# Reversed SSM tables by eight whole copies, and a step of the table batches every 5.5 ticks in a macaron decoder layer

## The chip, the cores and the metric

The kernel runs on one core of one Trainium2 chip. The metric is the device time of one execution in microseconds (us). The engines are PE (TensorE, matmuls), DVE (VectorE), ACT (ScalarE), POOL (GpSimd) and SP (SyncE, which here only issues DMAs). Each engine works through its own instructions in order and waits on semaphores for the others.

## The reference, cut to what matters

One decoder layer on 1024 tokens of width 1024, all in f32:

```
x = x + 0.5 * g1 * swiglu(modulate(rms_norm(x), sh1, sc1), W_gate, W_up, W_down)      # FFN1, width 2816
b, c, v, u = split(modulate(rms_norm(x), sh2, sc2) @ w_in)
yA = b * conv3_causal(c * v)
yB = GLU(Re(C . state) + D * u)      # state_t = Abar * state_{t-1} + Bbar * u_t, 32 groups of 16 channels, 64 states
x = x + g2 * ([rms_norm(yA) | rms_norm(yB)] @ w_out)
x = x + 0.5 * g3 * swiglu(modulate(rms_norm(x), sh3, sc3), ...)                       # FFN2
y = rms_norm_final(x)
```

`Abar = exp(lambda * dt)` and `Bbar = (Abar - 1) / lambda * B` come from the inputs, so the tables that the SSM (state space) stage needs can be made long before that stage. The state recursion is done in blocks of 8 time steps, and needs the powers 0 to 8 of `Abar`, once in rising and once in falling order.

## The kernel before, in words

Every product in f32 is made of three matmuls on fp32r operands split in a high and a low part (`mm3`, one *tick*). ACT casts a weight tile to its high part, DVE subtracts to get the low part (`w<-raw,w`). FFN1 and FFN2 use a seven-product scheme for blocks of two by two: the eleven groups of FFN1 are named fa0 to fa10, and groups fa2 to fa10 run through `seven`, first its side g (gate), then its side u (up). A side is seven steps of twelve matmuls (four ticks) into PSUM banks in the order A, C, B, D, A, E, C. In the trace they are `fa8gA`, `fa8gC` and so on. DVE adds the banks up (`fa8gu`, `fa8gt`, `fa8ut`); the second C accumulates onto the first one's bank, so PE may begin it only when DVE has added the first C in (`fa3gt<-fa3gu,fa3gC`). At the end of side u some ten more additions make the group's products and their sums (X, Y, Z, W).

Work that isn't part of FFN1 itself lies in a generator, `side1`, which `clock.tick` moves on by one `yield` after every `clock.period` ticks. It makes, in this order, the seven-product operands, the bases of the SSM tables (`ssm_base`) and the tables in eight batches of four groups (`ssm_batch`):

- `ssm_base` has the powers of `Abar` in `pw` (128 partitions, 2 parts, 9 powers, 32 groups) and makes four tables from it, `tab0` to `tab3`. The lower and upper 64 partitions take different parts and signs. `tab0` and `tab1` are whole copies (64x288); `tab2` and `tab3` have the powers 7 to 0 in reverse, copied one power at a time (64x32). After each of the eight table halves stands a `yield`.
- `ssm_batch(b)` makes, on DVE, `bb`, `cl`, `bl` and the rotors `rot`/`rott`. `bl` is a product with `tab2`, to which `blt`, a product with `tab3`, is added. Later steps put two small groups of work on PE, `kp` (reads `bl` and `cl`) and `tp` (transposes `bl`), and evacuate them (`kc`, `mi`). Each batch has 15 DMAs on SP: its parameters `prm`, and stores to `mo_d`, `co_d`, `si_d`, `mk_d` (eight) and `mi_d`. The batches also take eight `wm` tiles of the modulation along, all of them near the first one.

The period is 4.5 ticks from group fa2 on (`clock.period = 4.5`). When group fa10 begins, what is left of `side1` is run off, its buffers are closed, and the x tiles for the residual take their place (`load_x`); so the x loads wait for the last batch's stores. After FFN1's first half of the down projection the period is set to 8.

The rows of most instructions carry line L108, that of a recording wrapper; they are told apart by their tile names. The order of instructions on each engine is set by a scheduler from data dependences and its own estimates, in the neighbourhood of where they were written.

Of the kernel before, what the change touches and what calls it, by code (L numbers as in the profile page):

```python
# [13 lines left out]
F32 = mybir.dt.float32  # L14
F32R = mybir.dt.float32r
I32 = mybir.dt.int32
AF = mybir.ActivationFunctionType
# [4 lines left out]
P = 128  # L22
# [8 lines left out]
G = 32  # L31
# [201 lines left out]
def hymba_layer(ctx: ExitStack, tc, x_d, wm1_d, wmod_d, gu1_d, gs1_d, ds1_d, wl1_d, win_d, wout_d, glu_d, gu2_d, gs2_d, wd2_d, ds2_d, wl2_d, cols_d, cond_d, lam_d, bc_d, out_d):  # L233
    nc = tc.nc
    V, A, T, SP = (InOrder(tc, e) for e in (nc.vector, nc.scalar, nc.tensor, nc.sync))
# [82 lines left out]
    clock = Clock(4)  # L318
# [143 lines left out]
    def mod_fetch(home):  # L462
        if home is not None:
            n, b, i = later.pop(0)
            r = home(f"wm{n}_{b}_{i}")
            SP.dma_start(r, wmod_d[n - 2, b, :, i, :])
            fetched.append((n, 2 * b + i, r))
# [350 lines left out]
    for h in range(2):  # L818
# [7 lines left out]
        q = sqs[0]  # L826
# [94 lines left out]
    def ssm_base(sb, sb1):  # L921
# [102 lines left out]
        pw = sb1.tile([P, 2, 9, G], F32, tag="pw", name="pw")  # L1024
# [10 lines left out]
        yield  # L1035

        tabs = [sb.tile([P, 9, G], F32, tag=f"tab{i}", name=f"tab{i}") for i in range(4)]
        for n, (t, (top, ts_, bot, bs_)) in enumerate(zip(tabs, ((0, 1, 1, -1), (1, -1, 0, -1), (0, 1, 1, 1), (1, -1, 0, 1)))):
            for part, i, sg in ((lo, top, ts_), (hi, bot, bs_)):
                if n < 2:  # L1040
                    A.activation(t[part], pw[part, i], AF.Copy, scale=float(sg))
                else:

                    for q in range(8):
                        A.activation(t[part, q, :], pw[part, i, 7 - q, :], AF.Copy, scale=float(sg))
                yield
        zero = sb1.tile([CH, 112], F32, name="zero")
        V.memset(zero[:], 0.0)
        mk4 = mk_d[:].rearrange("b p (g c) -> p b g c", g=GB)
# [105 lines left out]
    def combos1():  # L1155

        sh = mods[:, 0, :]
        both = const.tile([P, 4], F32, name="both")
        V.tensor_tensor(out=both[:], in0=sh[:, :4], in1=sh[:, 4:], op=ALU.add)
        blocks.clear()  # L1160
        blocks.update(A11=act1[0][:4], A12=act1[0][4:], A22=act1[1][4:], S1=[], S2=[], S3=[], S4=[])
        for k in range(4):
            (t11, t21), (t12, t22) = x[k], x[4 + k]
            V.scalar_tensor_tensor(out=t22, in0=t22, scalar=both[:, k : k + 1], in1=t21, op0=ALU.add, op1=ALU.add)
            blocks["S1"].append(split_act(t22, f"h1S1_{k}", "B"))
            yield
            V.tensor_tensor(out=t21, in0=t11, in1=t21, op=ALU.subtract)
            blocks["S3"].append(split_act(t21, f"h1S3_{k}", "B"))
            yield
            V.scalar_tensor_tensor(out=t11, in0=t22, scalar=sh[:, k : k + 1], in1=t11, op0=ALU.subtract, op1=ALU.subtract)  # L1170
            blocks["S2"].append(split_act(t11, f"h1S2_{k}", "B"))
            yield
            V.scalar_tensor_tensor(out=t12, in0=t12, scalar=sh[:, 4 + k : 5 + k], in1=t11, op0=ALU.add, op1=ALU.subtract)
            yield
        while not left_free:
            yield
        for k in range(4):
            blocks["S4"].append(split_act(x[4 + k][0], f"h1S4_{k}", "A"))
            yield
        xp_open.close()  # L1180
        first_opened()

    def side1():
        yield from combos1()
        sb = side_open.enter_context(tc.tile_pool(name="sb", bufs=1, side="right"))
        with tc.tile_pool(name="sb1", bufs=1, side="right") as sb1:
            yield from ssm_base(sb, sb1)
        bps.append(side_open.enter_context(tc.tile_pool(name="bp", bufs=1, side="right")))
        mod_home.pool = side_open.enter_context(tc.tile_pool(name="wmp", bufs=1, side="right"))
        for _ in range(2):  # L1190
            mod_fetch(mod_home)
        for b in range(NB):
            yield from ssm_batch(b)
# [20 lines left out]
    def gate_up(act, name, kept, last):  # L1214

        afs = {}
        for fi in range(2):
            if last and fi:
                wg, wu = ws.take(2)
                for h in (1, 0):  # L1220
                    pg, pu = proj(wg, act[h], f"{name}g{fi}_{h}"), proj(wu, act[h], f"{name}u{fi}_{h}")
                    gu_keep(fi, h, pg, pu, afs, kept, name)
                    if h:
                        left_free.append(True)
                        clock.period = LAST_PERIOD
                ws.free(2)
# [7 lines left out]
            ws.free()  # L1234

    movs["B"] = es1.enter_context(tc.tile_pool(name="movB1", bufs=12))
    LAST_PERIOD = 2
    sums_open, first_open = ExitStack(), ExitStack()

    def first_opened():  # L1240
# [2 lines left out]
    ws.sums_pool = sums_open.enter_context(tc.tile_pool(name="sums", bufs=2))  # L1243
    ws.pump()
    clock.side.append(side1())
    clock.period = 3.5
    for g in range(1, SEVEN_FROM[0]):
# [483 lines left out]
```

## Time and profile before

| | |
|---|---|
| median of 3 runs | 1735.42 us (1735.38 to 1735.46) |
| the profiled execution, its own time | 1740.78 us |
| its span in the trace | 1739.0 us |
| mean granted TensorE clock | 0.987 |
| PE busy | 1665.4 us, 96% of the span |
| DVE busy | 1273.6 us, 73% |
| ACT busy | 596.7 us, 34% |
| POOL busy | 375.9 us, 22% |

A row of the timeline has the start in us from the span's begin, the length in us, the engine, the line, the operation, outputs and inputs by the program's names, the shape, and how many instructions are merged in the row; in square brackets, where the engine stood idle ahead of it, for how long and what ended that. Lengths of neighbouring rows overlap by about 0.1 us, so paces are taken from start to start. Busy shares are means over stages with different limits; FFN1, where the change lies, fills the trace from about 50 to 725 us.

### The profile page before, as it was taken

Reading aid. Unit: us, or ns where it says so; the run is one execution under the profiler, and the core shown is the slowest. Engines: PE = TensorE matmul, PEld = TensorE weight load, DVE = VectorE, ACT = ScalarE, POOL = GpSimd, SP = SyncE. Lnnn points to the kernel's source line nnn. Section 1 sums busy time; section 2 is a strip of 40 time slices with the busy share of each in tenths; the row PEclk is TensorE's granted clock in tenths of the full one; section 3 lists DMA queues with packets and bytes.
Section 4 is the critical chain, followed back from the end, with each engine's and each line's share of the span. In section 5 each row is a group of like instructions: output and inputs, shape, how many; then the busy total and the mean of one; then the engine's idle time right before and its main releaser. Section 6 shows DMA issues by size and latency. Waiting matters only on the chain.

```text
span 1739.0 us, 20621 instructions
## 1 busy us (share of the span) xinstructions
PE 1665.4 (96%) x7484; PEld 1368.4 (79%) x7484; DVE 1273.6 (73%) x2014; ACT 596.7 (34%) x1016; POOL 375.9 (22%) x290
## 2 busy tenths in 40 slices
PE   4999999999999999999999999999999999999997
PEld 3787788878878878787777778778888888888886
DVE  7939699997589997634556977967777766676656
ACT  4225433333364332331113414424444443322221
POOL 0012233322322222100000022123223322333211
PEclk9999999999999999999999999999999999999998
DMA  8222464554464656134655450114445334659312
GB/s 326 78 99 91 146 217 150 158 183 150 182 224 147 230 198 238 53 98 142 198 152 155 134 182 25 49 49 157 167 187 186 152 145 170 248 236 365 119 49 97
DMA packets 98167, 275.17 MB, mean 158 GB/s; under 512 B 18961, under 2 KB 34577, under 8 KB 86930
## 3 DMA queue, kind: packets, MB, share of 16 engines
q1 hardware_dynamic: 98066, 273.86, 44.8%
q8 instruction: 59, 0.97, 0.2%
q14 instruction: 42, 0.34, 0.1%
HBM read 194.65 MB, written 74.97 MB: 155 GB/s over the span
## 4 chain that ended last, share of the span: by engine, by line
PE 46%; DVE 7%; DMA 3%; issue 1%; ACT 0%; SPq 0%; POOL 0%; DVEq 0%; ACTq 0%
PE wo L108 2%; PE fb10d L108 2%; PE u L108 2%; PE fbd_1B L108 2%; PE fbd_0B L108 2%; PE b L108 2%; DMA swz<-si 1%; PE v L108 1%; PE fb0g L108 1%; PE fbd_1C L108 1%; PE fbd_0C L108 1%; PE fbd_1A L108 1%; PE fbd_0A L108 1%; DVE x L108 1%; DMA wm<-in_wmod 1%; PE gl L108 1%
## 5 line engine op out<-in xcount | busy, mean ns | idle before, releaser
L108 ACT CAST w<-raw 128x512 fp32r<-128x512 f32 (+1 forms) x374 | 240.4, 677 | 475.8 <-issue 79.4
L108 DVE TENSOR_TENSOR w<-raw,w 128x512 fp32r<-128x512 f32 (+1 forms) x374 | 306.6, 839 | 122.3 <-ACT w L108 121.7
L174 POOL TENSOR_TENSOR raw<-sums,raw 128x512 f32<-128x512 f32 x54 | 80.4, 1490 | 416.4 <-DVE w L108 404.0
L165 POOL TENSOR_TENSOR sums<-raw 128x512 f32<-128x512 f32 x54 | 77.4, 1434 | 335.5 <-DMA raw<-in_gs 140.8
L176 POOL TENSOR_TENSOR raw<-raw 128x512 f32<-128x512 f32 x54 | 84.7, 1571 | 96.5 <-DVE w L108 96.5
L166 POOL TENSOR_TENSOR raw<-raw 128x512 f32<-128x512 f32 x54 | 85.3, 1579 | 4.2
L108 DVE CUSTOM_DVE_ANT_0 wm<-wm,cact 128x1024 f32<-128x1024 f32 x56 | 77.6, 1398 | 10.6 <-DMA wm<-in_wmod 10.5
L367 POOL TENSOR_TENSOR n3aq<-n3aq,n3aq 128x512 f32<-128x512 f32 x5 | 7.7, 1530 | 281.3 <-ACT n3aq L108 281.1
L108 PE MATMUL p<-h,w 128*128 128x512 f32 x192 | 48.5, 415 | 8.2 <-DVE h L108 5.4
L108 DVE TENSOR_TENSOR w<-sums,w 128x512 fp32r<-128x512 f32 x54 | 52.7, 988 | 3.0 <-ACT w L108 2.4
L108 PEld LDWEIGHTS p<-h,w 128*128 128x128 f32 x192 | 38.4, 202 | 18.0 <-DVE h L108 6.4
L108 PE MATMUL wo<-oa,w 128*128 128x512 f32 x192 | 46.0, 392 | 1.2 <-DVE w L108 0.7
L108 PE MATMUL v<-h,w 128*128 128x512 f32 x192 | 46.8, 395 | 0.0
L108 PE MATMUL c<-h,w 128*128 128x512 f32 x192 | 46.6, 394 | 0.0
L108 PE MATMUL u<-h,w 128*128 128x512 f32 x192 | 46.3, 401 | 0.2 <-DVE h L108 0.2
L108 PE MATMUL b<-h,w 128*128 128x512 f32 x192 | 45.6, 393 | 0.0
L108 PE MATMUL wo<-ob,w 128*128 128x512 f32 x192 | 45.3, 391 | 0.0
L108 ACT CAST w<-sums 128x512 fp32r<-128x512 f32 x54 | 32.8, 620 | 35.2 <-PE fa9gE L108 2.2
L108 PEld LDWEIGHTS u<-h,w 128*128 128x128 f32 x192 | 36.7, 193 | 8.6 <-DVE h L108 0.6
L108 PEld LDWEIGHTS wo<-oa,w 128*128 128x128 f32 x192 | 35.7, 188 | 9.6 <-DVE w L108 1.1
L108 PEld LDWEIGHTS wo<-ob,w 128*128 128x128 f32 x192 | 35.8, 188 | 7.3
L108 PEld LDWEIGHTS b<-h,w 128*128 128x128 f32 x192 | 35.5, 188 | 7.2
(1576 smaller groups left out, 4013.1 us busy)
## 6 DMA issues: line engine op xcount, KB each, us to landing
raw<-in_gs SPq DMA_DIRECT2D x38, 1024.0 KB, 5.2
wm<-in_wmod SPq DMA_DIRECT2D x56, 512.0 KB, 4.8
raw<-in_ds SPq DMA_DIRECT2D x16, 1024.0 KB, 6.0
mw<-in_wm SPq DMA_DIRECT2D x8, 1024.0 KB, 12.8
x<-in_x SPq DMA_DIRECT2D x16, 512.0 KB, 8.5
raw<-in_win SPq DMA_DIRECT2D x8, 1024.0 KB, 5.1
raw<-in_gu SPq DMA_DIRECT2D x6, 1024.0 KB, 10.0
raw<-in_wl SPq DMA_DIRECT2D x5, 1024.0 KB, 6.5
```

The source lines that it names most:

```text
L108: r = getattr(self.engine, name)(*args, **kw)
L165: self.G.tensor_tensor(out=f, in0=r[2], in1=r[1], op=ALU.subtract)
L166: self.G.tensor_tensor(out=r[1], in0=r[1], in1=r[0], op=ALU.subtract)
L174: self.G.tensor_tensor(out=r, in0=s["t3"], in1=r, op=ALU.add)
L176: self.G.tensor_tensor(out=r, in0=self.chunk(j, 3), in1=r, op=ALU.subtract)
L367: nc.gpsimd.tensor_tensor(out=a, in0=a, in1=sq[:, :n], op=ALU.add)
```

## The change

In `ssm_base` the falling powers are first copied whole, both parts and all partitions at once, into a new tile `pd` (eight copies of 128x2x32, a `yield` after the fourth and the eighth). Then `tab2` and `tab3` take their halves from it in one instruction each (64x256, four in all). A `yield` stands behind each table, no longer behind each half, so the tables have six of them (two of the copies) in place of eight. When `ssm_base` is through, `side1` sets the period to 5.5 ticks for the batches.

```diff
         tabs = [sb.tile([P, 9, G], F32, tag=f"tab{i}", name=f"tab{i}") for i in range(4)]
+        down_ = sb1.tile([P, 2, 8, G], F32, tag="pd", name="pd")
+        for q in range(8):
+            A.copy(down_[:, :, q, :], pw[:, :, 7 - q, :])
+            if q % 4 == 3:
+                yield
         for n, (t, (top, ts_, bot, bs_)) in enumerate(...):
             for part, i, sg in ((lo, top, ts_), (hi, bot, bs_)):
                 if n < 2:
                     A.activation(t[part], pw[part, i], AF.Copy, scale=float(sg))
                 else:
-                    for q in range(8):
-                        A.activation(t[part, q, :], pw[part, i, 7 - q, :], AF.Copy, scale=float(sg))
-                yield
+                    A.activation(t[part, 0:8, :], down_[part, i], AF.Copy, scale=float(sg))
+            yield
...
             yield from ssm_base(sb, sb1)
+        clock.period = BATCH_PERIOD
...
-    LAST_PERIOD = 2
+    LAST_PERIOD, BATCH_PERIOD = 2, 5.5
```

How that changes the order of the built program, at three places. First ACT in side g of group fa3, where the tables are made. `w_1344` and `w_1400` are weight tiles that are cast, `fa3gt` is the side's activation. Before:

```order
L108 ACTIVATE tab_1523<-pw 64x288
L108 ACTIVATE tab_1524<-pw 64x288
L108 ACTIVATE tab_1523<-pw 64x288
L108 CAST w_1344<-raw_1039 128x512
L108 CAST w_1344<-raw_1165 128x512
L108 ACTIVATE tab_1524<-pw 64x288
L108 ACTIVATE tab_1525<-pw 64x32 x16
L108 ACTIVATE tab_1526<-pw 64x32 x16
L108 CAST w_1400<-raw_1165 128x512 x2
L108 ACTIVATE fa3gt_1321<-fa3gt_1321 128x512
```

and after:

```order
L108 ACTIVATE tab_1523<-pw 64x288
L108 ACTIVATE tab_1524<-pw 64x288
L108 COPY pd<-pw 128x2x32 x2
L108 CAST w_1344<-raw_1039 128x512
L108 CAST w_1344<-raw_1165 128x512
L108 COPY pd<-pw 128x2x32 x6
L108 ACTIVATE tab_1523<-pw 64x288
L108 ACTIVATE tab_1524<-pw 64x288
L108 ACTIVATE tab_1525<-pd 64x256 x2
L108 ACTIVATE tab_1526<-pd 64x256 x2
L108 CAST w_1400<-raw_1165 128x512 x2
L108 ACTIVATE fa3gt_1321<-fa3gt_1321 128x512
```

The casts keep their places; between `w_1344` and `w_1400` stand 12 instructions where there were 33.

Second, DVE around the seventh batch's `bl`. The rows from the end of group fa7 (`fa7Y`) to the last addition into `bl_3172`, before:

```order
L108 TENSOR_TENSOR fa7Y<-fa7uu_3025,fa7gu_2837 128x512
L108 TENSOR_TENSOR cl_3140<-tab_1523,prm_3131 128x576
L108 TENSOR_TENSOR clt_3141<-tab_1524,prm_3131 128x576
L108 TENSOR_TENSOR fa7W<-fa7Y,fa7W 128x512
L108 TENSOR_TENSOR w_3158<-raw_2822,w_3158 128x512 x2
L108 TENSOR_TENSOR cl_3140<-cl_3140,clt_3141 128x576
L108 TENSOR_TENSOR w_3205<-raw_2822,w_3205 128x512
L108 TENSOR_TENSOR bl_3172<-tab_1525,bb_3133 128x512
L108 TENSOR_TENSOR w_3205<-raw_2986,w_3205 128x512
L108 TENSOR_TENSOR blt_3173<-tab_1526,bb_3133 128x512
L108 TENSOR_TENSOR fa8gu_3232<-fa8gt_3182,fa8gB 128x512
L108 TENSOR_TENSOR bl_3172<-bl_3172,blt_3173 128x512
```

The seventh batch's `bl_3284` after, half a group on, behind the last addition of side g of fa8:

```order
L108 TENSOR_TENSOR fa8gu_3151<-fa8gu_3151,fa8gC 128x512
L108 TENSOR_TENSOR cl_3257<-cl_3257,clt_3258 128x576
L108 TENSOR_TENSOR bl_3284<-tab_1525,bb_3250 128x512
L108 TENSOR_TENSOR w_3290<-raw_2911,w_3290 128x512
L108 TENSOR_TENSOR blt_3285<-tab_1526,bb_3250 128x512
L108 TENSOR_TENSOR w_3290<-raw_2911,w_3290 128x512
L108 TENSOR_TENSOR bl_3284<-bl_3284,blt_3285 128x512
```

It is now the sixth batch whose `bl` lies around the end of group fa7: its first product `bl_3103` stands behind `fa7Y`, seven rows of the end of the group follow, and then, after:

```order
L108 TENSOR_TENSOR fa7W<-fa7Y,fa7W 128x512
L108 TENSOR_TENSOR blt_3104<-tab_1526,bb_3064 128x512
L108 TENSOR_TENSOR rot_3141<-rs,rt_1444 128x512
L108 TENSOR_TENSOR w_3125<-raw_2753,w_3125 128x512
L108 TENSOR_TENSOR w_3125<-raw_2911,w_3125 128x512
L108 TENSOR_TENSOR bl_3103<-bl_3103,blt_3104 128x512
```

The fourth batch (end of fa6) and the eighth (end of fa8) lie the same way after the change; before, only the seventh did.

Third, PE at the seventh batch's `kp`. Before it stands in step D of side g of fa8:

```order
L108 MATMUL fa8gD<-h1S_0_656,w_3074 128x512 x3
L108 MATMUL fa8gD<-h1S_1_722,w_3074 128x512 x3
L108 MATMUL fa8gD<-h1S_2_793,w_3074 128x512 x3
L108 MATMUL kp_3244<-cl_3140,bl_3172 16x128 x4
L108 MATMUL tp_3249<-ident,bl_3172 128x128 x4
```

and after at the end of the second step A of side u:

```order
L108 MATMUL fa8uA<-h_0_440,w_3237 128x512 x3
L108 MATMUL fa8uA<-h_0_477,w_3237 128x512 x3
L108 MATMUL fa8uA<-h_0_509,w_3237 128x512 x3
L108 MATMUL kp_3375<-cl_3257,bl_3284 16x128 x4
L108 MATMUL tp_3380<-ident,bl_3284 128x128 x4
```

The sixth batch's `kp` moves from the first three matmuls of step E of fa7's side u to those of step E of fa8's side g, the eighth's from the second step A of fa8's side u to the end of the second step A of fa9's side g.

## The prediction, made before the changed kernel was run

> **What bounds the kernel now.** I read the page first, then the busy time by stretches, then TensorE in order of time, row by row, through FFN1, since that is where the diff acts.
>
> ```profile
> PE 1665.4 (96%) x7484; PEld 1368.4 (79%) x7484; DVE 1273.6 (73%) x2014; ACT 596.7 (34%) x1016; POOL 375.9 (22%) x290
> ```
>
> PE is the bound, so only PE's holes can be won. The next view gives busy time by stretch (columns: stretch, length, then PE, PEld, DVE, ACT, POOL, the granted clock, the DMA share and GB/s).
>
> ```profile
> 348.00:391.00 43.00, 39.12 (x182) 31.12 (x181) 39.33 (x62) 13.12 (x24) 11.37 (x8) 0.94 0.57 182
> 435.00:478.00 43.00, 43.00 (x191) 35.63 (x190) 21.81 (x32) 14.67 (x27) 15.32 (x11) 1.00 0.47 182
> ```
>
> While the table batches run, DVE is busy 39.3 of 43 us. After the last of them it needs 21.8 of 43, and PE has no hole. In the timeline of PE between 165 and 495 us exactly two rows carry an idle time. The first (the bracket is idle time and who ended it):
>
> ```profile
> 181.37 2.88 PE L108 MATMUL fa3gE<-h,w 128*128 128x512 f32 x12
> 187.73 4.57 PE L108 MATMUL fa3gC<-h1S,w 128*128 128x512 f32 x12 [3.48 <-DVE fa3gt L108]
> 192.13 2.90 PE L108 MATMUL fa3uA<-h,w 128*128 128x512 f32 x12
> 194.87 2.88 PE L108 MATMUL fa3uC<-h1S,w 128*128 128x512 f32 x12
> ```
>
> Twelve matmuls take 2.72 us from start to start (370.27 to 372.99 in a fence below), so fa3gC could have begun at 181.37 + 2.72 = 184.09. It began 3.64 late and then took 4.40 (187.73 to 192.13) instead of 2.72, 1.68 more: **5.3 us** lost. The second hole, and an undisturbed batch to hold it against:
>
> ```profile
> 348.07 1.52 PE L108 MATMUL fa7gC<-h1S,w 128*128 128x512 f32 x6
> 349.53 1.05 PE L108 MATMUL kp<-cl,bl 128*16 128x128 f32 x8
> 350.50 0.66 PE L108 MATMUL tp<-ident,bl 128*128 128x128 f32 x4
> 350.91 1.62 PE L108 MATMUL fa7gC<-h1S,w 128*128 128x512 f32 x6
> 352.37 2.88 PE L108 MATMUL fa7uA<-h,w 128*128 128x512 f32 x12
> ...
> 381.15 2.20 PE L108 MATMUL fa8gD<-h1S,w 128*128 128x512 f32 x9
> 387.24 1.86 PE L108 MATMUL kp<-cl,bl 128*16 128x128 f32 x8 [3.88 <-DVE bl L108]
> 389.03 1.12 PE L108 MATMUL tp<-ident,bl 128*128 128x128 f32 x4
> 389.80 1.63 PE L108 MATMUL fa8gD<-h1S,w 128*128 128x512 f32 x3
> 391.23 3.77 PE L108 MATMUL fa8gA<-h,w 128*128 128x512 f32 x12
> 394.83 2.89 PE L108 MATMUL fa8gE<-h,w 128*128 128x512 f32 x12
> ```
>
> A step of twelve with a batch's kp and tp inside takes 352.37 - 348.07 = 4.30, so kp and tp cost 1.58. From 381.15 to 394.83 stand 13.68 us where 4.30 + 2.72 = 7.02 would do: **6.66 us** lost, of them some 4.05 waiting and 2.6 in slow matmuls behind it. Both holes together are 12.0.
>
> **Term 1, the tables.** Removed: 32 ACT instructions of 64x32. Added: 8 copies of 128x2x32 and 4 of 64x256; the four of 64x288 stay. ACT's rows:
>
> ```profile
> 166.43 0.39 ACT L108 COPY rs<-kk 128x256 f32<-128x256 f32 x1
> 166.72 0.62 ACT L108 CAST w<-raw 128x512 fp32r<-128x512 f32 x1
> ...
> 178.72 1.23 ACT L108 ACTIVATE tab<-pw 64x288 f32<-64x288 f32 x3 [5.25 <-DVE pw L108]
> 179.98 1.14 ACT L108 CAST w<-raw 128x512 fp32r<-128x512 f32 x2
> 181.02 4.60 ACT L108 ACTIVATE tab<-pw 64x288 f32<-64x288 f32 x33
> 185.64 1.14 ACT L108 CAST w<-raw 128x512 fp32r<-128x512 f32 x2
> ```
>
> and what stands behind them on DVE:
>
> ```profile
> 186.29 0.69 DVE L108 TENSOR_TENSOR w<-raw,w 128x512 fp32r<-128x512 f32 x1 [2.84 <-ACT w L108]
> 186.90 0.68 DVE L108 TENSOR_TENSOR fa3gt<-fa3gu,fa3gC 128x512 f32<-128x512 f32 x1
> ```
>
> So the 33 instructions (4.62 us to the next start) hold up a weight cast, DVE stands 2.84 us at the subtraction that needs it, the bank's addition fa3gt is queued behind that, and PE waits for fa3gt. The order rows show the same chain after the change: in the place of the 33 come 6 copies, 2 of 64x288 and 4 of 64x256, then the same casts. Paces from start to start: 0.29 for 128x256 (166.43 to 166.72), 0.52 for 128x512 (1.04 for two at 179.98), hence about 0.32 for 288 columns; 0.134 for 32 columns ((4.62 - 0.32)/32). The trace has no copy of 2x32. It lies between 0.134 and 0.29; I take 0.16, since 64 columns are near 32. That makes 6 x 0.16 + 2 x 0.32 + 4 x 0.29 = 2.76, 1.86 less than 4.62. At 0.29 a copy, and 0.42 (1.26/3) for each wide one, it would be 4.26, only 0.36 less. Before the cast at 179.98 stand two wide ones and two copies instead of three wide ones: at 0.96 against 1.26 another 0 to 0.3; I take 0.2. So fa3gC starts 2.0 earlier (0.4 to 2.2) and still waits about 1.6. The two new waits (copies on pw, the table rows on the copies) stay on ACT, in its own order; DVE's rows in this place are the same ones. What the 1.68 behind the hole becomes hangs on the clock:
>
> ```profile
> 1131.37 3.02 PE L108 MATMUL fb0d<-fb_0a,w 128*128 128x512 f32 x12 [2.06 <-DVE x L108]
> 1140.03 5.97 PE L108 MATMUL fb0d<-fb_1a,w 128*128 128x512 f32 x18 [1.87 <-DVE x L108]
> ...
> 1131.40:1135.00 3.60, 2.99 (x12) 2.15 (x12) 3.60 (x7) 0.62 (x1) 0.00 (x0) 1.00 0.00 0
> 1140.00:1143.00 3.00, 2.97 (x8) 2.33 (x9) 3.00 (x5) 0.62 (x1) 0.44 (x1) 0.58 0.00 0
> ```
>
> A hole of 2.06 us was followed by full clock (3.02 for twelve against the usual 2.88), one of 1.87, nine us later and after that first hole, by a granted clock of 0.58. A lone hole of 1.6 after dense work is nearer to the first, so I take full clock and 0.1 behind it: term 1 is 2.0 + 1.6 = **3.6** (2.0 if the clock drops, 0.4 at the slow end of the copies).
>
> The Trainium skill (TensorE: Matmul & The Clock Gate, Part 1, What's actually happening) states that the clock halves after at least one idle window of some 3.4 us. By that rule 1.6 us never costs a clock, and the sum stays at 10.3. The row at 1140.03 does not agree: 1.87 us, and 0.58.
>
> **Term 2, the batches at every 5.5 ticks in place of 4.5.** No instruction is added or removed; the kp and tp of eight batches still cost 8 x 1.58 on PE. What changes is how far DVE runs behind when PE reaches a kp:
>
> ```profile
> 347.15 1.67 DVE L108 TENSOR_TENSOR bl<-bl,blt 128x512 f32<-128x512 f32 x1
> ...
> 374.12 0.67 DVE L108 TENSOR_TENSOR fa7uu<-fa7uu,fa7uE 128x512 f32<-128x512 f32 x1
> ...
> 385.34 0.68 DVE L108 TENSOR_TENSOR fa8gu<-fa8gt,fa8gB 128x512 f32<-128x512 f32 x1
> 385.94 1.16 DVE L108 TENSOR_TENSOR bl<-bl,blt 128x512 f32<-128x512 f32 x1
> ```
>
> The fifth batch's bl ends at 348.82, 0.7 ahead of its kp at 349.53; the seventh's ends at 387.1, 3.9 after PE could have begun (381.15 + 9/12 x 2.72 = 383.19). DVE is late there: it adds bank E at 374.12, though PE had finished E at 370.27 (next fence). After the change I go by the order, DVE at 0.60 a row (385.34 to 385.94) and up to 1.1 more for a row that runs long, as 347.15 does (1.67 against some 0.6); all places of after are on the clock of before without term 1's shift. Anchors on PE:
>
> ```profile
> 370.27 2.88 PE L108 MATMUL fa7uC<-h1S,w 128*128 128x512 f32 x12
> 372.99 2.88 PE L108 MATMUL fa8gA<-h,w 128*128 128x512 f32 x12
> ...
> 400.28 2.88 PE L108 MATMUL fa8uA<-h,w 128*128 128x512 f32 x12
> ...
> 411.16 2.65 PE L108 MATMUL fa8uA<-h,w 128*128 128x512 f32 x11
> ...
> 478.06 2.88 PE L108 MATMUL fa10uA<-h,w 128*128 128x512 f32 x12
> ```
>
> and one of the queue that issues the loads:
>
> ```profile
> 445.40 0.33 SPq L108 DMA_DIRECT2D raw<-in_gs  x1
> ```
>
> Seventh batch: its kp moves from fa8gD to the end of the second fa8uA, 411.16 + 2.72 - 6.66 - 1.58 = 405.6 (the hole gone, one batch fewer ahead of it). Its bl is the seventh DVE row from fa8gC's addition, which may start at 400.28 - 8.24 = 392.0; 7 x 0.6 and two long rows end by 398.5, 7 us ahead. Tightest is the sixth: fa7uE ends at 370.27 - 1.58 = 368.7, 17 DVE rows later (10.2, with three long rows 13.5) bl is done by 382.2; its kp, behind three matmuls of fa8gE, stands at 372.99 - 1.58 + 5 x 2.72 + 0.68 = 385.7, 3.5 ahead. Next on DVE is fa8gt, six rows on (385.8), due when fa8gC starts at 385.0 + 2.72 + 1.58 = 389.3. So I take the second hole as gone: **6.66** (bounds 0 and 6.66). The eighth batch's kp moves 12 us on, to the end of fa9g's second A (405.6 + 1.58 + 7 x 2.72 = 426.2), into the stretch where DVE was busy half the time. Every batch takes its loads and stores along on SP, and the weight loads (raw) stand between them. The one that moves most is the last of fa10: it was issued at 445.40, and now stands behind the eighth batch's stores and the first x load. Its weights are first used in fa10uA, 33 us later (478.06), so some us there cost nothing. POOL has no part in the steps; that its sums of weights lengthen a DVE row is in the 1.1 above.
>
> **Sum.** 3.6 + 6.66 = 10.3. The profiled execution took 1740.78 us (span 1739.0 and 1.8 around it), 5.4 above the median of 1735.42; against its own time it would be 1730.5, against the median **1725.1**, if the timed runs have the same two holes.
>
> **Rivals.** (a) All as above, but the clock drops behind the shorter hole as at 1140.03: 8.7 gained, 1726.7. (b) Only one term pays: a batch still makes PE wait once, or the seventh's wait, which an unprofiled run may not have (the fifth missed one by 0.7), is no loss to remove: 3.6 gained, 1731.8. For it speaks that DVE's lag is a matter of single us; against, that every margin I find is over 3. (c) No difference: DVE still misses, and the copies of 2x32 run at the slow end, 0.4 gained, 1735.0. (d) Slower: before, one batch alone had the row blt and the closing bl behind the ten additions that end a group on DVE, and that one stalled. In the new order the fourth, sixth and eighth all have it. If DVE is over 3.5 us behind when the u side ends (it was 3.85 at the seventh batch before, 370.27 to 374.12), each stalls as that one did: 3 x 6.66 against 10.3 gained, 1745.1. Against it: DVE has 17 us from fa7uE's end to kp where before it had 383.19 - 370.27 = 12.9.
>
> **How the numbers follow.** As forecast 45%, (a) 25%, (b) 16%, (c) 9%, (d) 5%. What a measurement can tell from no change is 0.2%, 3.5 us; (b) stands just at that edge, so half of it counts as same, and some of (c)'s as well: faster 0.79, same 0.16, slower 0.05. The range goes from both holes wholly gone (12.0 gained, 1723.4, rounded down to 1723) to just past (b), 1732, which leaves out about 14%. Of the forecast and (a) alone it would be 1723 to 1728.
>
> **What would show it.** Right: fa3gC idle 1 to 2 us instead of 3.48, ACT's block of tables near 2.8 us, every kp without idle time, DVE below 90% in the stretches up to 435. Wrong: an idle time ahead of a kp or of an fa7, fa8 or fa9 gC, released by DVE; a granted clock below 1 behind fa3gC (case a); or the copies of 2x32 at 0.3 us.

## The result, and the profile after

The changed kernel's median is 1732.49 us (1731.0 to 1737.24, 21 runs, the profiled one among them) against 1738.95 (1735.24 to 1745.57, 21 runs) of the kernel before on the same chip: ratio 0.9961, 95% interval 0.9952 to 0.9971, about 6.8 us. A second comparison, on record below, gave 0.9959 (0.9945 to 0.9973). The forecast was 10.3 us and 1725.1, the range 1723 to 1732; the time lies just above it. The forecast started from the median of three runs, 1735.42; over 21 runs the kernel before has 1738.95, 3.5 more. The profiled execution took 1736.77 us (span 1735.0, mean granted clock 0.989) against 1740.78 (1739.0, 0.987).

The page's first line and the two stretches that were shown of before (columns: stretch, length, PE, PEld, DVE, ACT, POOL, granted clock, DMA share, GB/s):

```profile
PE 1665.9 (96%) x7484; PEld 1369.3 (79%) x7484; DVE 1279.4 (74%) x2014; ACT 595.8 (34%) x996; POOL 373.1 (22%) x290
```

```profile
348.00:391.00 43.00, 43.00 (x207) 34.80 (x206) 41.01 (x64) 16.10 (x29) 12.30 (x9) 1.00 0.52 167
435.00:478.00 43.00, 43.00 (x192) 35.59 (x191) 24.04 (x34) 14.94 (x27) 12.09 (x9) 1.00 0.57 204
```

PE has no hole left in the stretch that held the seventh batch's wait (207 matmuls where 182 fitted before), although DVE is fuller there than before (41.0 of 43). The timeline of PE at the sixth batch's kp, and DVE's closing bl and fa8gt around it:

```profile
387.99 0.84 PE L108 MATMUL fa8gE<-h,w 128*128 128x512 f32 x3
388.76 1.05 PE L108 MATMUL kp<-cl,bl 128*16 128x128 f32 x8
...
408.70 1.05 PE L108 MATMUL kp<-cl,bl 128*16 128x128 f32 x8
```

```profile
383.30 0.69 DVE L108 TENSOR_TENSOR bl<-bl,blt 128x512 f32<-128x512 f32 x1
...
402.15 0.69 DVE L108 TENSOR_TENSOR bl<-bl,blt 128x512 f32<-128x512 f32 x1
```

The sixth's bl ends at 383.99, 4.8 us ahead of kp (forecast: 3.5); the seventh's at 402.84, 5.9 ahead (forecast: 7). The first hole, at fa3gC, shrank less than forecast:

```profile
183.39 2.88 PE L108 MATMUL fa3gE<-h,w 128*128 128x512 f32 x12
188.56 3.00 PE L108 MATMUL fa3gC<-h1S,w 128*128 128x512 f32 x12 [2.29 <-DVE fa3gt L108]
191.39 2.88 PE L108 MATMUL fa3uA<-h,w 128*128 128x512 f32 x12
```

fa3gC could have begun at 183.39 + 2.72 = 186.11; it began 2.45 late and lost 0.11 more behind: 2.56 lost where it was 5.3. DVE still waits for ACT's weight cast ahead of fa3gt, 1.74 us where it was 2.84:

```profile
187.12 0.69 DVE L108 TENSOR_TENSOR w<-raw,w 128x512 fp32r<-128x512 f32 x1 [1.74 <-ACT w L108]
187.73 0.68 DVE L108 TENSOR_TENSOR fa3gt<-fa3gu,fa3gC 128x512 f32<-128x512 f32 x1
```

And side g of group fa5 has a hole that was not there before:

```profile
263.69 2.88 PE L108 MATMUL fa5gE<-h,w 128*128 128x512 f32 x12
268.42 4.55 PE L108 MATMUL fa5gC<-h1S,w 128*128 128x512 f32 x12 [1.85 <-DVE fa5gt L108]
272.77 2.98 PE L108 MATMUL fa5uA<-h,w 128*128 128x512 f32 x12
```

It began 2.01 late (against 263.69 + 2.72 = 266.41) and took 4.35 to the next start, with a granted clock of 0.71 in the first 2.6 us of it: 2.01 + 4.35 - 2.72 = 3.6 us lost. DVE's rows there show why, before:

```profile
263.52 0.68 DVE L108 TENSOR_TENSOR fa5gu<-fa5gu,fa5gD 128x512 f32<-128x512 f32 x1
264.12 0.69 DVE L108 TENSOR_TENSOR w<-raw,w 128x512 fp32r<-128x512 f32 x1
264.73 0.68 DVE L108 TENSOR_TENSOR fa5gt<-fa5gu,fa5gC 128x512 f32<-128x512 f32 x1
...
265.93 0.21 DVE L108 TENSOR_TENSOR dg<-ident,lam 16x64 f32<-16x64 f32 x1
```

and after:

```profile
259.01 1.23 DVE L108 CUSTOM_DVE_ANT_0 wm<-wm,cact 128x1024 f32<-128x1024 f32 x1
...
263.03 0.21 DVE L108 TENSOR_TENSOR dg<-ident,lam 16x64 f32<-16x64 f32 x1
...
264.33 0.76 DVE L108 TENSOR_TENSOR cl<-tab,prm 128x576 f32<-128x576 f32 x1
265.00 0.75 DVE L108 TENSOR_TENSOR clt<-tab,prm 128x576 f32<-128x576 f32 x1
265.67 0.68 DVE L108 TENSOR_TENSOR fa5gu<-fa5gu,fa5gD 128x512 f32<-128x512 f32 x1
266.27 1.41 DVE L108 TENSOR_TENSOR w<-raw,w 128x512 fp32r<-128x512 f32 x1
267.60 0.68 DVE L108 TENSOR_TENSOR fa5gt<-fa5gu,fa5gC 128x512 f32<-128x512 f32 x1
```

The second batch's first rows (dg to clt, 2.6 us) now stand ahead of fa5gt instead of behind it, just after the first batch's two reductions of wm. The subtraction in front of fa5gt is also long here, 1.41 in place of 0.69.

By these three places the change is worth 6.66 + (5.32 - 2.56) - 3.64 = 5.8 us in this profile. The stretch that holds them shows it: from the start of fa3gE to that of fa10uC it is 495.21 - 181.37 = 313.84 us before and 492.43 - 183.39 = 309.04 after, 4.8 less, and 5.75 less without the wait ahead of fa10uC, which is 1.62 us after and 0.67 before. The spans differ by 4.0 only; part of the rest is fa2uC, which waits 1.68 us after and 0.99 before. These two waits (at 164.96 and 495.21 us before) lie just outside the stretch of 165 to 495 us in which the prediction found exactly two holes. In the second profile of the changed kernel fa2uC waits 0.48 us and fa10uC not at all, so such differences come from one execution to the next.

### The profile page after: what moved, and what is told of

The parts are those of the page before. It is cut to its first block, busy times and chain, and to the rows that moved or that the text cites. A ratio compares the mean times of both kernels' runs of the same rounds, so it can differ in the third digit from the quotient of the medians.

```text
span 1735.0 us, 20600 instructions
## 1 busy us (share of the span) xinstructions
PE 1665.9 (96%) x7484; PEld 1369.3 (79%) x7484; DVE 1279.4 (74%) x2014; ACT 595.8 (34%) x996; POOL 373.1 (22%) x290
## 4 chain that ended last, share of the span: by engine, by line
PE 46%; DVE 7%; DMA 3%; issue 1%; ACT 0%; SPq 0%; POOL 0%; DVEq 0%; ACTq 0%
PE wo L108 2%; PE fb10d L108 2%; PE u L108 2%; PE fbd_1B L108 2%; PE fbd_0B L108 2%; PE v L108 2%; PE b L108 2%; DMA swz<-si 1%; PE fb0g L108 1%; PE fbd_1C L108 1%; PE fbd_0C L108 1%; PE fbd_1A L108 1%; PE fbd_0A L108 1%; DVE x L108 1%; PE gl L108 1%; DMA wm<-in_wmod 1%
## 5 line engine op out<-in xcount | busy, mean ns | idle before, releaser
L108 DVE TENSOR_TENSOR w<-raw,w 128x512 fp32r<-128x512 f32 (+1 forms) x374 | 311.9, 854 | 115.7 <-ACT w L108 114.9
```

The lines of the kernel that those rows point to most:

```text
L108: r = getattr(self.engine, name)(*args, **kw)
```

## The experiments

All ratios are to the kernel before, in alternating runs, each comparison on one chip; 0.001 is 1.74 us.

**The two missing yields.** The tables got eight yields again:

```diff
                 else:
                     A.activation(t[part, 0:8, :], down_[part, i], AF.Copy, scale=float(sg))
+                if part is hi and n >= 2:
+                    yield
             yield
```

> The changed kernel with one thing put back: a yield behind each half of tab2 and tab3, so that the tables have eight yields again as before, and the batches begin 9 ticks later. On DVE the second batch's first rows (dg, bb, cl) then stand behind fa5gt instead of ahead of it. Theory A (each hole counts by itself; the two missing yields made the new hole at fa5gC): no idle time ahead of fa5gC, the fa3gC hole stays near 2.5 us of loss, kp without idle; 2.8 + 6.7 = 9.4 us gained over the kernel before, ratio about 0.9946, that is 3.7 us faster than the changed kernel. Rival B (what is won at fa5gC is lost again later, at the C additions of fa6 to fa9, which now have six to nine batch rows ahead of them): ratio 0.996 as the changed kernel, with a new idle time at one of those. Rival C (the hole at fa5gC is in the profiled execution alone): no idle time there in this profile either, but the ratio stays at 0.996.

Ratio **0.9951** (0.9937 to 0.9965; median 1729.8). The timeline of PE has no idle time at fa5gC, and none at the C additions of fa6 to fa9:

```profile
264.95 1.62 PE L108 MATMUL fa5gE<-h,w 128*128 128x512 f32 x6
266.41 2.88 PE L108 MATMUL fa5gC<-h1S,w 128*128 128x512 f32 x12
```

```profile
264.19 0.68 DVE L108 TENSOR_TENSOR fa5gt<-fa5gu,fa5gC 128x512 f32<-128x512 f32 x1
...
265.39 0.21 DVE L108 TENSOR_TENSOR dg<-ident,lam 16x64 f32<-16x64 f32 x1
```

Rival B falls by these rows. Rival C falls by the other profiles with six yields, the second one of the changed kernel among them, which all have the hole (below). The interval overlaps that of the changed kernel, so the gain of 1.7 us is not shown by this run alone. In fa3g the pause was nearly the same as in the changed kernel's profile, but this time the clock fell behind it:

```profile
186.95 4.39 PE L108 MATMUL fa3gC<-h1S,w 128*128 128x512 f32 x12 [2.32 <-DVE fa3gt L108]
```

**The period alone.** The kernel before with `clock.period = BATCH_PERIOD` for the batches, nothing else.

> The kernel before with the period of 5.5 ticks for the batches alone: the 32 small ACT instructions and the eight yields of the tables stay. Theory A: the seventh batch's hole goes (6.7 us), fa3gC keeps its loss of 5.3, fa5gC has none because fa5gt stays ahead of the second batch's rows: ratio about 0.9962, as much as the whole change brings. Rival B (the gain is that of the tables, the period moves the hole elsewhere): ratio 0.999 to 1.001. Rival C (the hole at fa5gC comes from the period, not from the missing yields): an idle time of 1.5 to 2 us ahead of fa5gC here too, ratio about 0.998.

Ratio **0.9961** (0.9945 to 0.9978), as theory A has it. Every kp is without idle time, fa5gC too, and fa3gC is as in the kernel before:

```profile
188.72 4.58 PE L108 MATMUL fa3gC<-h1S,w 128*128 128x512 f32 x12 [3.49 <-DVE fa3gt L108]
```

**The tables alone.** The changed kernel without that line.

> The changed kernel without the period of 5.5: the new tables with their six yields, batches at every 4.5 ticks, which begin 9 ticks earlier than before. Theory A: 2.8 us gained at fa3gC; an idle time ahead of fa5gC as in the changed kernel (3.7 lost, more if the closing row of cl, which now also stands ahead of fa5gt, adds its 0.7); the seventh kp, now in fa8gB at some 381 us, still waits, since its bl stands 15 rows behind the addition of fa7uE that came at 374: 0 to 6.7 us. Together between 6 gained and 1 lost, likeliest 1 to 3 gained, ratio 0.998 to 0.9995. Rival B (the tables bring the gain): 0.996.

Ratio **1.0006** (0.9992 to 1.002): no gain, at the bad end of theory A's range; the 1 to 3 us that it called likeliest did not come. Besides what the timeline of PE shows here, fa8uC waits 1.43 us:

```profile
185.69 3.01 PE L108 MATMUL fa3gC<-h1S,w 128*128 128x512 f32 x12 [2.29 <-DVE fa3gt L108]
...
265.84 4.58 PE L108 MATMUL fa5gC<-h1S,w 128*128 128x512 f32 x12 [2.13 <-DVE fa5gt L108]
...
383.87 1.03 PE L108 MATMUL kp<-cl,bl 128*16 128x128 f32 x8 [2.55 <-DVE bl L108]
```

**The yields alone.** The period of 5.5 and the old tables, but six yields (`if n > 1 or part is hi: yield`).

> The period of 5.5 ticks for the batches with the old tables (32 instructions of 64x32), but with six yields for the tables in place of eight, as in the changed kernel: the only difference from the run with the period alone is two yields. Its DVE order around fa5gt is the changed kernel's. Theory A (the two yields alone put the second batch's rows ahead of fa5gt): an idle time of 1.5 to 2.2 us ahead of fa5gC comes back with the old tables, 2.0 to 3.7 us lost with what the clock does behind it, fa3gC idle 3.5; ratio about 0.9975 (0.9970 to 0.9983), against 0.9961 of the period alone. Rival B (the new tables' instructions make the hole at fa5gC): none there, ratio 0.9961.

Ratio **0.9982** (0.9964 to 0.9999). The hole at fa5gC is there with the old tables; this time the clock held, so it cost 1.8 us:

```profile
270.41 2.98 PE L108 MATMUL fa5gC<-h1S,w 128*128 128x512 f32 x12 [1.51 <-DVE fa5gt L108]
```

Against the period alone, two yields less cost 0.0021 with the old tables, and 0.0010 with the new ones (0.9961 against 0.9951). Neither difference is clear of its intervals. The hole itself follows the yields in all twelve traces, though: it stands in the five with six yields (idle 1.51 to 2.13) and in none of the seven with eight, with old and new tables. That the yields make it is shown; its price is known to some 2 us.

**Why the wide instructions took 0.42.** tab2 and tab3 in the order lower, lower, upper, upper half.

```diff
+        for part, k in ((lo, 1), (hi, 3)):
+            for t, s4 in spec[pair_ : pair_ + 2]:
```

> The changed kernel with tab2 and tab3 made in the order lower half of both, then upper half of both, instead of lower, upper, lower, upper. Everything else on ACT stands as in the changed kernel. Theory (two neighbouring 64-partition instructions on different halves can't overlap, which is why the wide ones took 0.42 us from start to start where 128x256 takes 0.29): the second of each pair starts 0.29 to 0.32 after the first, the four take 1.4 in place of 1.68. Rival (a 64-partition instruction of 256 columns takes 0.42 wherever it stands, or they wait for what they read): 0.42 for all four.

One execution, 1727.78 us. ACT's four wide instructions, each in a row of its own, of the changed kernel and then of this one:

```profile
184.76 0.40 ACT L108 ACTIVATE tab<-pd 64x256 f32<-64x256 f32 x1
185.17 0.42 ACT L108 ACTIVATE tab<-pd 64x256 f32<-64x256 f32 x1
185.60 0.42 ACT L108 ACTIVATE tab<-pd 64x256 f32<-64x256 f32 x1
186.03 0.41 ACT L108 ACTIVATE tab<-pd 64x256 f32<-64x256 f32 x1
```

```profile
183.35 0.42 ACT L108 ACTIVATE tab<-pd 64x256 f32<-64x256 f32 x1
183.68 0.40 ACT L108 ACTIVATE tab<-pd 64x256 f32<-64x256 f32 x1
184.09 0.42 ACT L108 ACTIVATE tab<-pd 64x256 f32<-64x256 f32 x1
184.41 0.40 ACT L108 ACTIVATE tab<-pd 64x256 f32<-64x256 f32 x1
```

On the same partitions the next starts after 0.33 and 0.32, on the other half after 0.41 to 0.43, with no overlap at all. The theory holds in these rows; it is worth 0.2 us here. In the run below with the wide instructions doubled the built program still alternates the halves, and the eight start 0.42 to 0.44 apart, as the theory has it.

**ACT's block shorter, and longer.** The eight copies alone, or these and the four wide instructions, on POOL (both with eight yields); and the four wide ones done twice:

```diff
-            A.copy(down_[:, :, q, :], pw[:, :, 7 - q, :])
+            nc.gpsimd.tensor_copy(down_[:, :, q, :], pw[:, :, 7 - q, :])
...
-                    A.activation(t[part, 0:8, :], down_[part, i], AF.Copy, scale=float(sg))
+                    nc.gpsimd.tensor_scalar(out=t[part, 0:8, :], in0=down_[part, i], scalar1=float(sg), scalar2=None, op0=ALU.mult)
```

> As the last, but only the eight copies into pd on POOL; the four wide instructions stay on ACT. Theory A: ACT's block is 1.3 us shorter than in the changed kernel (eight copies of 0.16), unless it now waits for POOL's copies: if eight of them take over 2 us on POOL, the four wide ones start late and nothing is won. fa3gC idle 1.0 in the first case, 2.3 or more in the second. Rival B: idle near 2.3 whatever ACT does.

> The reversed tables taken off ACT: the eight copies into pd and the four wide instructions run on POOL, with eight yields as before and the period of 5.5. Between the two weight casts in fa3g ACT has one 64x288 left. Theory A (fa3gC waits for that cast through DVE, us for us): the cast comes 2.4 us and more earlier, fa3gC idle 0 to 0.7 in place of 2.3, no clock drop behind it; with the seventh kp's hole gone and none at fa5gC about 11.5 us gained, ratio 0.9930 to 0.9940. Rival B (DVE itself or a weight that POOL now delivers later holds fa3gC): idle still near 2 us, ratio 0.995 as with the eight yields alone; POOL's sum of weights behind the tables (due near 187 us) may then show as the releaser of a cast.

> The changed kernel with eight yields, and the four wide instructions of tab2 and tab3 done twice: four more of 64x256 ahead of the weight cast. If ACT's block sets fa3gC: 1.3 us more where a pair on the same partitions starts 0.32 apart, 1.7 where each takes 0.42; idle 3.6 to 4.0 ahead of fa3gC against 2.3, and, as behind every idle time of about 3.5 there so far, the clock drops and the twelve matmuls take 4.4. If DVE's own rows set it: idle stays near 2.3.

The timeline of PE, copies on POOL, all on POOL, wide ones doubled (a single execution each for the first and the last, 1732.02 and 1734.03 us):

```profile
184.71 2.97 PE L108 MATMUL fa3gC<-h1S,w 128*128 128x512 f32 x12 [0.92 <-DVE fa3gt L108]
```

```profile
185.79 2.98 PE L108 MATMUL fa3gC<-h1S,w 128*128 128x512 f32 x12 [0.86 <-DVE fa3gt L108]
```

```profile
189.50 5.46 PE L108 MATMUL fa3gC<-h1S,w 128*128 128x512 f32 x12 [4.71 <-DVE fa3gt L108]
```

ACT's block does set fa3gC: 1.3 us less on ACT took 1.4 off the pause. Taking the 1.7 of the wide ones off ACT as well brought nothing more, because DVE is then the limit; its rows with all on POOL run without a gap up to fa3gt:

```profile
183.76 0.69 DVE L108 TENSOR_TENSOR fa3gu<-fa3gu,fa3gD 128x512 f32<-128x512 f32 x1
184.36 0.68 DVE L108 TENSOR_TENSOR w<-raw,w 128x512 fp32r<-128x512 f32 x1
184.96 0.68 DVE L108 TENSOR_TENSOR fa3gt<-fa3gu,fa3gC 128x512 f32<-128x512 f32 x1
```

So theory A of the run with all on POOL was right on the direction and wrong on an idle time of 0 to 0.7. Doubling added 1.76 on ACT and 2.4 to the pause, which is 4.71 where 3.6 to 4.0 was expected; 0.6 of the 2.4 is the subtraction in front of fa3gt, which took 1.32 on DVE in place of 0.69. All on POOL has ratio **0.9941** (0.9919 to 0.9963), where 0.9930 to 0.9940 was expected. It was run again beside the changed kernel:

> The changed kernel unaltered, beside the next one on the same chip: ratio 0.9961 (0.9952 to 0.9971) as before if the first comparison holds. By the sum of holes: at fa3gC 2.8 us less loss than the kernel before where the clock stays, 1.2 less where it drops; 6.7 gained at the seventh kp; 2.0 to 3.7 lost at fa5gC.

> The reversed tables on POOL with eight yields and the period of 5.5, unaltered, to be held against the changed kernel on one chip. Theory A (holes add up): fa3gC 0.9 idle, no hole at fa5gC, so 2.0 to 3.7 us at fa5gC and 1.4 to 3.0 at fa3gC better than the changed kernel: 3.4 to 6.7 us faster, ratio to the kernel before 0.9925 to 0.9941. Rival: the 0.9941 measured first was the favourable end and it is no better than the eight yields alone, 0.9951.

0.9959 (0.9945 to 0.9973) and **0.9943** (0.9930 to 0.9956): some 2.8 us better than the changed kernel, less than the 3.4 to 6.7 of theory A, and the lowest ratio of all versions. The two intervals overlap, and so does that of the eight yields alone (0.9951), so the order of the three is likely and not shown. Medians 1731.91 and 1728.6.

## Why the prediction was right and wrong

**Right: term 2's main point.** The period of 5.5 removes the seventh batch's wait. Every kp is free of idle time, and the period alone gives 0.9961, 6.8 us, where 6.66 was forecast (the interval runs from 3.8 to 9.6). Rivals (c) and (d) are out. The last load of fa10, which moved most, is not named in any wait there; ahead of fa10uC, ACT waits for a load of the down projection (`raw<-in_ds`), before (2.81 us) as after (3.32).

**The step that failed: "every margin I find is over 3".** Only the kp and fa8gt were worked out, and "what would show it wrong" named the C additions of fa7 to fa9. The change also takes two yields from the tables, so the first batches start 9 ticks earlier; at fa5 that puts 2.6 us of batch rows ahead of fa5gt. The sum has no term for that. It costs 1.8 us where the clock holds (second profile of the changed kernel, idle 1.55) and 3.6 where it drops.

**Mis-sized: term 1.** The copies of 2x32 were priced right (six in 183.95 - 182.96 = 0.99, 0.165 each against 0.16). The four wide ones were priced at the 128x256 pace, 0.29, and took 0.43 each (186.47 - 184.76 = 1.71), and the two 64x288 took 0.81 in place of 0.64. ACT's rows:

```profile
182.96 0.97 ACT L108 COPY pd<-pw 128x64 f32<-128x64 f32 x6
183.95 0.90 ACT L108 ACTIVATE tab<-pw 64x288 f32<-64x288 f32 x2
184.76 1.68 ACT L108 ACTIVATE tab<-pd 64x256 f32<-64x256 f32 x4
186.47 1.14 ACT L108 CAST w<-raw 128x512 fp32r<-128x512 f32 x2
```

3.51 us, not 2.76, so the pause is 2.29 us and not 1.6. The 0.42 stood in the term as its upper end; the row that it came from, x3 of 64x288, was the nearer one. The Trainium skill (ScalarE: Activation LUTs, What ACT_TABLE_LOAD costs) gives, for tiles of 128 partitions, 186 ns + 0.833 ns per element and an overlap of 93 ns between neighbours. For 256 elements that is an estimate of 0.40, with which the lengths of these rows of 64 partitions agree (0.40 to 0.42); the overlap the rows show only on the same partitions (0.42 long, the next start after 0.33).

**Neither right nor wrong: the clock behind fa3gC.** Full clock was forecast, with rival (a) for the drop. Of five profiles with a pause of 2.08 to 2.32 us there, two have the drop. So term 1 is worth 5.32 - 2.56 = 2.8, or 1.2 where the clock drops, in place of 3.6. The timed runs don't resolve it: with eight yields the new tables have 0.9951 and the old ones 0.9961, with overlapping intervals. The holes add up to 6.66 + 2.76 - 3.64 = 5.8 us in the first profile of the changed kernel and to 6.66 + 1.24 - 1.81 = 6.1 in the second; 6.8 was measured. The 6.66 is from the one profile of the kernel before.

**The base, too low by 3.5.** The 10.3 was taken off 1735.42, the median of three runs, though the profiled execution took 5.4 more. Of the 7.4 us between 1725.1 and the measured 1732.49, 3.5 are this base and 3.9 the gain. Either alone would have left the time inside the range: 1738.95 - 10.3 = 1728.6, and 1735.42 - 6.8 = 1728.6. Why those three runs were among the fastest is not shown. So it is by chance that the price of rival (b), 1731.8, lies close to the measured median. Its mechanism is not what the profiles show: both holes shrank, and a third took part of it back.

**Wrong on the way:** DVE below 90% up to 435 us. It was busy 41.0 of 43 us from 348 to 391 (39.3 before), while PE came further in the same time; a full DVE cost nothing where nobody waited for the rows.

## What to carry to other kernels

When side work is moved in time, go through every place where the main work waits on the shared engine, from the first moved row to the last, not only through the wait that the move is to remove; the new wait came in a group that had none, from two yields that looked like bookkeeping. Price an instruction by the pace of its own shape, and take the rows that are already in the trace over a wider neighbour. And count a pause of PE by its length first; what the clock adds is a matter of chance for pauses near 2 us, so one profile can't settle it. Take the base from as many runs as the result is measured with: three runs were off by 3.5 us here, half of the whole gain.

## What the runs showed of the hardware

**Pauses of TensorE and the clock.** Over the twelve profiles, ahead of the second C steps of FFN1: of 29 pauses up to 1.75 us none was followed by slow matmuls; of eight between 1.85 and 2.54 us five were; of the four of 3.47 and more all were. The same pause of 2.04 to 2.07 us ahead of fb0d had slow matmuls behind it in six of twelve executions. In the first row below 18 matmuls run 6.00 us where 18 / 12 x 2.72 = 4.1 is the usual pace; in the second twelve run 3.02:

```profile
1128.63 6.00 PE L108 MATMUL fb0d<-fb_0a,w 128*128 128x512 f32 x18 [2.06 <-DVE x L108]
```

```profile
1122.34 3.02 PE L108 MATMUL fb0d<-fb_0a,w 128*128 128x512 f32 x12 [2.06 <-DVE x L108]
```

Both rows are of the changed kernel, in two profiles. The Trainium skill (TensorE: Matmul & The Clock Gate, Part 1, What's actually happening) says that the activity window runs freely and does not start with the kernel; that the same pause costs in one execution and not in the next is what one would expect of it, though no run here shows the window itself. Its condition, at least one idle window of some 3.4 us, does not agree: a pause of 1.85 us was enough.

**What the spread goes with.** In the 42 runs of the kernel before in two of the comparisons, those with a mean granted clock of 0.987 took 1741.8 us on average (six runs), those with 0.991 1734.9 (three): 1.7 us for each 0.001. A longer time goes with a lower clock; what lowers it in an execution, beyond the pauses above, is not shown. The medians of 21 runs differ by 6.5 us, the two profiled spans by 4.0.

**POOL's copies.** Eight copies of 2x32 columns took 1.57 us on POOL, not much more than on ACT (8 x 0.165 = 1.3); the four 64x256 products took 4.19 there against 1.71 on ACT.
